# Transposes between the products of the second pair, and where the block sums of layer 0 run, in a two-layer hybrid decoder

## The chip, the cores and the metric

The kernel runs on one core of one Trainium2 chip. The metric is the device time of that core in microseconds; the time before is the median of three runs. A profile of one further execution comes with it. In the profile PE is TensorE, DVE is VectorE, ACT is ScalarE, POOL is GpSimd, SP is SyncE (here a DMA queue). L234 is line 234 of the kernel before.

## What is computed

A trunk of two layers over 1024 tokens of width 1024, in float32. Layer 0 mixes tokens with an RG-LRU block, layer 1 with RWKV-7; each mixer is followed by a cross-attention into 256 memory tokens and by a squared-ReLU MLP:

```python
def reference(x, mem, ...):
    mem_n = rms_norm(mem, mem_norm)
    for i in range(DEPTH):
        g = ln_gains[i]
        hn = rms_norm(x, g[0])
        t = rglru_mixer(hn, ...) if i % N_MIXERS == 0 else rwkv7_mixer(hn, ...)
        x = x + rms_norm(t, g[1])
        c = mem_cross_attention(rms_norm(x, g[2]), mem_n, c_w_q[i], c_w_kv[i], c_w_o[i])
        x = x + rms_norm(c, g[3])
        m = sqrelu_mlp(rms_norm(x, g[4]), m_w_up[i], m_w_down[i])
        x = x + rms_norm(m, g[5])
    return x

def mem_cross_attention(h, mem_n, w_q, w_kv, w_o):
    q = (h @ w_q).reshape(B, S, MEM_HEADS, MEM_HEAD_DIM)
    ...

def sqrelu_mlp(h, w_up, w_down):
    return jnp.square(jax.nn.relu(h @ w_up)) @ w_down
```

## The kernel before

**Arithmetic.** Each float32 product is made of three matmuls on operands that are split in a high and a low half (`mm3`, L314 to L320: high by high L318, high by low L319, low by high L320). A split (`split`, L228 to L235) is a cast on ACT (L233) and a subtraction on DVE (L234) for the low half; of a whole unit of 128 x 1024 it is one instruction of each.

**Phases.** A projection whose result leaves with tokens on the partitions is a `tphase`: eight token tiles of 128, for each one 48 matmuls of 512 columns, then `post`, which runs the tail (post-norm, residual, pre-norm of the next block: L327 on ACT, L329 and L331 on POOL, L647, L648 and L655 on DVE). The pre-normed tiles are collected in `xs`; when four are there, a step that transposes them is put into `self.later`, and `catch_up` runs what waits there.

**The 7-product projections.** The query projections of both layers (`c_w_q`, 4 pairs of output tiles) and the up projections of both MLPs (`m_w_up`, 16 pairs) go through `cphase`. It takes the activations as 2 x 2 blocks and computes a pair with seven products of 12 matmuls each instead of eight. `combine_in` makes the operands from the activations: for each half `hf` of the tokens it transposes four tiles, eight groups `k` of four transposes (L384), evacuates each group with the norm's gain (L387 on DVE for k = 1 and 3, L389 on ACT), and splits blocks. The half `hf` = 0 gives b11 and b21. With `hf` = 1 come the block sums t1 = b12 - b11, t2 = b22 - t1, t3 = b11 - t2 and t4 = b21 - t2 (L415; two units each, so eight subtractions) and the splits of t1, t2, t3, b22 and t4. `combine_w` makes the four weight sums of a pair on POOL (L433, L434) and splits them. `make` does that ahead of time: the tphase of a cross-attention calls it behind its tiles 4 and 5 (`MAKE`), so that the MLP's first two pairs find their weights made.

`begin` runs p1 (with b11, into the bank x, copied by ACT, L474) and p2 (with b21, into z, added by DVE, L476). `finish` takes the made weights or calls `combine_w`. The first two pairs run in `together`: begin and finish of both, then `mid`, then p5, p6, p7, p3 and p4, each for both pairs. p5 reads t1, p6 t2, p7 t3, p3 b22 and p4 t4; p6 and p5 are copied by ACT (L485, L490), p7 and p3 added by DVE (L494, L498). For the first two pairs `mid` is `second_half`: it changes the PSUM layout to two pools of four banks and calls `catch_up`, which runs `combine_in` for `hf` = 1, 32 transposes and all sums.

**Layer 0's query projection is different.** There `xattn` first runs the rest of `memkv` (keys and values of layer 1's memory: each step 48 matmuls of 256 columns, with two splits of weights). `self.held` is a list then, and `combine_in` puts the five steps t1, t2, t3, b22, t4 into it, with the subtractions on POOL; after each of five `memkv` steps one of them is run.

**Order.** The program is written out once; the framework then puts each engine's instructions in order by a planner, by program order among those that it reckons ready. Tiles come from pools: 45 units of 128 x 1024 in SBUF (`BUFS`), PSUM banks by `bank(n)`, which takes pool n modulo the number of pools. Weights are fetched in the order of a plan; `depth` and `ahead` say how many units are split and loaded ahead, and loads go through SP's queue (L245 for pairs of projection weights, L253 for rows).

Of the kernel before, what the change touches and what calls it, by code (L numbers as in the profile page):

```python
# [9 lines left out]
AF = mybir.ActivationFunctionType  # L10
ALU = mybir.AluOpType
# [16 lines left out]
MAKE = (4, 5)  # L28
D = 1024
KT = 8  # L30
# [19 lines left out]
class Net:  # L50
# [322 lines left out]
    def combine_in(self, xs, hf, g, B):  # L373

        nc = self.nc
        raw = B.setdefault("raw", {})
        for k in range(KT):
            if k % 2 == 0:
                t = raw[hf, k // 2] = self.unit()
                pair = self.halves()  # L380
            o = slice((k % 2) * 512, (k % 2) * 512 + 512)
            p = pair[k % 2]
            for i, x in enumerate(xs):
                nc.tensor.transpose(p[:, i * 128:i * 128 + 128], x[:, k * 128:k * 128 + 128], self.ident)  # L384
            gc = self.colt[:, g + k:g + k + 1]
            if k in (1, 3):
                nc.vector.tensor_scalar(t[:, o], p, gc, None, ALU.mult)  # L387
            else:
                nc.scalar.activation(t[:, o], p, AF.Copy, scale=gc)  # L389

        def parts(name, ts, big=False):
            if big:
                z = self.half_big([4, 1024], F32R)
                st = [z[:, i, :] for i in range(4)]
            else:
                st = [self.unit(F32R) for _ in range(4)]
            for i, t in enumerate(ts):
                self.split(t, st[i], st[2 + i])
            at = lambda o, k: st[o + k // 2][:, (k % 2) * 512:(k % 2) * 512 + 512]
            B[name] = [(at(0, k), at(2, k)) for k in range(4)]  # L400

        r = lambda h, j: [raw[h, 2 * j + i] for i in range(2)]
        if hf == 0:
            parts("b11", r(0, 0), True)
            parts("b21", r(0, 1), True)
            return
        b11, b21, b12, b22 = r(0, 0), r(0, 1), r(1, 0), r(1, 1)
        del B["raw"]
        t2 = []

        def sums(name, to, x, y):
            if name == "t2":
                to.extend(self.unit() for _ in range(2))
            for o, m, n in zip(to, x, y):
                eng.tensor_tensor(o, m, n, ALU.subtract)  # L415
            parts(name, to)

        eng = nc.vector if self.held is None else nc.gpsimd
        steps = [lambda: sums("t1", b12, b12, b11), lambda: sums("t2", t2, b22, b12), lambda: sums("t3", b11, t2, b11),
                 lambda: parts("b22", b22), lambda: sums("t4", b21, b21, t2)]  # L420
        if self.held is None:
            for step in steps:
                step()
        else:
            self.held += steps

    def combine_w(self, two, first):

# [30 lines left out]
    def cphase(self, w, n, B, func, evac, then=None, ahead=2):  # L459

        nc = self.nc
        a, b = slice(0, 512), slice(512, 1024)
        st = {}


        place = lambda i: 0 if i < ahead else (i + 1) % 2

        def begin(i):
            two, first = self.made[i][:2] if i in self.made else self.take(("w", w, i))
            h, l = first  # L470
            x, z = self.bank(place(i)), self.bank(place(i))
            c0, c1 = self.unit(), self.unit()
            self.product(x, (h[:, a], l[:, a]), B["b11"], True, False)
            nc.scalar.copy(c0[:, a], x)  # L474
            self.product(z, (h[:, b], l[:, b]), B["b21"], True, True)
            nc.vector.tensor_add(c0[:, a], c0[:, a], z)  # L476
            st[i] = x, c0, c1, two, first

        def finish(i):
            x, c0, c1, two, first = st[i]  # L480
            st[i] = x, [], c0, c1, self.made.pop(i)[2] if i in self.made else self.combine_w(two, first)

        def p6(x, y, c0, c1, A, at):
            self.product(x, A["s2"], B["t2"], False, False)
            nc.scalar.copy(c0[:, b], x)  # L485

        def p5(x, y, c0, c1, A, at):
            y.append(self.bank(1 if at < ahead else place(at)))
            self.product(y[0], A["s1"], B["t1"], True, False)
            nc.scalar.copy(c1[:, b], y[0])  # L490

        def p7(x, y, c0, c1, A, at):
            self.product(x, A["s3"], B["t3"], False, False)
            nc.vector.tensor_add(c1[:, b], c1[:, b], x)  # L494

        def p3(x, y, c0, c1, A, at):
            self.product(y[0], A["s4"], B["b22"], False, True)
            nc.vector.tensor_add(c0[:, b], c0[:, b], y[0])  # L498

        def p4(x, y, c0, c1, A, at):  # L500
            self.product(x, A["a22"], B["t4"], False, True)
            nc.scalar.activation(c1[:, a], x, func or AF.Copy)

        def end(i):
            c0, c1 = st.pop(i)[2:4]
            if func is not None:
                nc.scalar.activation(c0, c0, func)
                nc.scalar.activation(c1[:, b], c1[:, b], func)
            behind.append(evac(i, c0, c1))


        behind = []

        def rest():
            while behind:
                behind.pop(0)()


        def narrow(i):
            if i >= n - 2:  # L520
                self.depth, self.ahead = 2 * (n - 1 - i), 0

        def together(two, mid=lambda: None):
            for i in two:
                narrow(i)
                begin(i)
                finish(i)
                if then and i == n - 2:
                    then[0]()
            mid()  # L530
            for step in (p5, p6, p7, p3, p4):
                for i in two:
                    step(*st[i], i)
                if then and step is p7 and two[-1] == n - 1:
                    with self.behind():
                        then[1]()
            for i in two:
                end(i)

        def second_half():  # L540
            self.psum_layout("banks")
            self.catch_up()

        together(range(ahead), second_half)
        for i in range(ahead, n - 2 if then else n):
            narrow(i)
            begin(i)
            finish(i)
            rest()
            for step in (p6, p5, p7, p3, p4):  # L550
                step(*st[i], i)
            end(i)
        if then:
            together(range(n - 2, n), rest)
        return rest


# [314 lines left out]
    def xattn(self, layer, xt, post, mid):  # L872
# [13 lines left out]
        if layer == 0:  # L886

            self.memkv(1, 3)
            self.held = []
            self.catch_up()  # L890
            for _ in range(5):
                self.memkv(1, 1)
                self.held.pop(0)()
            self.held = None
        self.kv_flush()
        self.depth, self.ahead = UP
# [331 lines left out]
        yield from rwkv_lora_weights(self, parts, out[-1])  # L1228


def rwkv(self, X, xt, lw_wa, lw_g, post):
    nc, I = self.nc, self.I
    mm = nc.tensor.matmul
    hgd = self.dram([128, 1024])
# [13 lines left out]
    raw = self.unit()  # L1248
# [571 lines left out]
    for q in range(4):  # L1820
        for h in range(2):
            rows.append([w[(2 * q + pp) * 128 + h * 64:(2 * q + pp) * 128 + h * 64 + 64, :] for pp in range(2)])
    self.tphase(rows, lambda tt: z[tt], post)


def network(net, I, out):
    x = [I["x"][0]] + [net.dram([1024, 1024]) for _ in range(5)] + [out[0]]
    early = []
    g = lambda l, i: I["ln_gains"][l, i]
    net.memory()  # L1830
    net.memkv(0, START[0])
    net.cols_fill(net.nc.gpsimd, 256)
    xt = net.head(x[0], net.lncol(0, 0), beside=START[1:])
    net.memory_out()
    net.memkv(0, 8 - sum(START))
    net.cols_fill(net.nc.gpsimd, 328)
    post, nxt = net.tail(g(0, 1), x[0], x[1], net.lncol(0, 2), combine=True)
    net.rglru(xt, post)
    for l in range(2):
        if l == 1:  # L1840
            xt = nxt
            post, nxt = net.tail(g(1, 1), x[3], x[4], net.lncol(1, 2), combine=True)
            rwkv(net, raw, xt, *early, post)
        post, xt = net.tail(g(l, 3), x[3 * l + 1], x[3 * l + 2], net.lncol(l, 4), combine=True)
        net.xattn(l, nxt, post, lambda tt: tt in MAKE and net.make(I["m_w_up"][l], MAKE.index(tt)))
        raw = []
        if l == 0:
            post, nxt = net.tail(g(0, 5), x[2], x[3], net.lncol(1, 0), raw=raw)
        else:
            post, nxt = net.tail(g(1, 5), x[5], x[6], None, last=True)  # L1850
        net.mlp(l, xt, raw, post, [rwkv_early(net, early)] if l == 0 else None)
# [21 lines left out]
```

## Time and profile before

| | |
|---|---|
| median of 3 runs | 2918.43 us (2918.1 to 2918.5) |
| the profiled execution, its own time | 2919.01 us |
| its span, first to last instruction | 2917.3 us |
| mean granted TensorE clock | 0.987 |
| PE busy | 2810.0 us |
| DVE busy | 1844.2 us |
| ACT busy | 1421.5 us |
| POOL busy | 929.3 us |
| matmuls | 16955 |
| HBM traffic | 143 GB/s over the span |

A row of the timeline reads: start in us from the span's start, duration, engine, line, operation, output <- input by the program's names, shapes and count, and in brackets the idle time of the engine just before and what ended it. In a row of waits stand the waiting engine and line, whom it waited for, the sum in us, the times and the longest. In the view by stretches each row is a stretch, its length, then the busy time of each engine with the number of its instructions, the granted clock, the share of the DMA engines and GB/s. A group row gives line, engine, operation, shapes and count, then busy us and mean ns, then the idle time ahead of it. Matmuls overlap in the pipeline, so the pace is read from the distance between their starts, not from their durations.

### The profile page before, as it was taken

The page shows a single profiled execution, that of the slowest core. Times are in us where ns is not written, and L with a number is a line of the kernel's source. Part 1 is how long each engine was busy: PE and PEld are TensorE (multiplying, and loading weights), DVE is VectorE, ACT ScalarE, POOL GpSimd, SP SyncE. Part 2 cuts the span into 40 slices and gives each one's busy share as a digit, 9 for nine tenths or more (in the row PEclk, how much of TensorE's full clock was granted, in tenths as well). Part 3 has the DMA queues.
Part 4 walks back from the last instruction along what each step waited for, and adds up shares of the span by engine and source line. Part 5 has one row for each costly group of instructions (what it writes and reads, how often), then busy time and mean ns, then how long its engine had stood idle before and what let it go on. Part 6 is the DMA issues. An engine that isn't in the chain of part 4 may idle for free.

```text
span 2917.3 us, 42725 instructions
## 1 busy us (share of the span) xinstructions
PE 2810.0 (96%) x16955; PEld 2342.2 (80%) x16955; DVE 1844.2 (63%) x1987; ACT 1421.5 (49%) x2195; POOL 929.3 (32%) x970
## 2 busy tenths in 40 slices
PE   7999999999999999999999899999899999999998
PEld 6888788887888888887878677888688788888886
DVE  5577566657455577887676624773765645567778
ACT  6465354545444543347561534553554544454333
POOL 2000144023666500012287113851402376650001
PEclk9999999999999999999999999999999999999999
DMA  8212342323444654442657798952232354464443
GB/s 258 78 46 73 108 160 68 104 81 102 150 153 155 221 183 158 146 144 73 176 139 219 213 226 238 240 131 94 62 106 80 102 162 145 147 238 162 157 173 115
DMA packets 383591, 421.91 MB, mean 145 GB/s; under 512 B 91184, under 2 KB 294176, under 8 KB 383392
## 3 DMA queue, kind: packets, MB, share of 16 engines
q1 hardware_dynamic: 371360, 379.19, 43.2%
q0 software_dynamic: 11568, 39.41, 3.7%
q8 instruction: 133, 2.18, 0.3%
q14 instruction: 66, 0.54, 0.1%
q10 hardware_dynamic: 464, 0.59, 0.1%
HBM read 283.79 MB, written 134.74 MB: 143 GB/s over the span
## 4 chain that ended last, share of the span: by engine, by line
PE 81%; DVE 5%; DMA 4%; issue 4%; ACT 3%; POOL 3%; SPq 1%; DVEq 0%; POOLq 0%; ACTq 0%
PE q L318 16%; PE q L320 16%; PE q L319 16%; PE p L318 8%; PE p L320 8%; PE p L319 8%; DVE u L234 2%; DMA u<-d 1%; PE q L1642 1%; DMA u<-in_b_w_rkv 1%; ACT u L233 1%; POOL u L1401 1%; POOL w L1399 1%; PE q L1535 1%; PE q L384 1%
## 5 line engine op out<-in xcount | busy, mean ns | idle before, releaser
L234 DVE TENSOR_TENSOR u<-u,u 128x1024 fp32r<-128x1024 f32 (+1 forms) x594 | 817.5, 1409 | 363.9 <-ACT u L233 341.8
L233 ACT CAST u<-u 128x1024 fp32r<-128x1024 f32 (+1 forms) x594 | 582.3, 1019 | 426.3 <-DVE u L1032 224.7
L318 PE MATMUL q<-u,u 128*128 128x512 f32 (+2 forms) x1984 | 760.0, 386 | 13.8 <-ACT u L233 10.9
L319 PE MATMUL q<-u,u 128*128 128x512 f32 (+2 forms) x1984 | 760.4, 384 | 8.5 <-DVE u L234 7.7
L320 PE MATMUL q<-u,u 128*128 128x512 f32 (+2 forms) x1984 | 753.9, 383 | 0.8 <-DVE u L234 0.8
L318 PE MATMUL p<-u,u 128*128 128x512 f32 (+1 forms) x1472 | 557.2, 381 | 16.3 <-ACT u L233 5.6
L319 PE MATMUL p<-u,u 128*128 128x512 f32 (+1 forms) x1472 | 554.5, 377 | 3.9 <-DVE u L234 3.9
L320 PE MATMUL p<-u,u 128*128 128x512 f32 (+1 forms) x1472 | 552.5, 376 | 3.2 <-DVE u L234 3.2
L318 PEld LDWEIGHTS q<-u,u 128*128 128x128 f32 (+1 forms) x1984 | 373.9, 189 | 90.8 <-ACT u L233 13.0
L329 POOL TENSOR_SCALAR s<-s 128x1 f32<-128x1 f32 x98 | 40.0, 409 | 1273.4 <-ACT u L327 1271.9
L319 PEld LDWEIGHTS q<-u,u 128*128 128x128 f32 (+1 forms) x1984 | 374.3, 189 | 82.4 <-DVE u L234 10.8
L320 PEld LDWEIGHTS q<-u,u 128*128 128x128 f32 (+1 forms) x1984 | 374.2, 189 | 73.9 <-DVE u L234 1.0
L318 PEld LDWEIGHTS p<-u,u 128*128 128x128 f32 x1472 | 281.6, 191 | 70.3 <-ACT u L233 11.8
L319 PEld LDWEIGHTS p<-u,u 128*128 128x128 f32 x1472 | 281.7, 191 | 55.8 <-DVE u L234 7.0
L320 PEld LDWEIGHTS p<-u,u 128*128 128x128 f32 x1472 | 281.1, 191 | 54.7 <-DVE u L234 5.0
L433 POOL TENSOR_TENSOR u<-u,u 128x512 f32<-128x512 f32 x120 | 192.1, 1605 | 10.1 <-PE q L319 5.1
L1090 DVE TENSOR_TENSOR z<-z,q 128x512 f32<-128x512 f32 x192 | 130.4, 682 | 81.1 <-PE q L320 81.1
L320 PE MATMUL q<-z,u 128*128 128x512 f32 x320 | 124.9, 392 | 3.9 <-DVE u L234 3.9
L319 PE MATMUL q<-z,u 128*128 128x512 f32 x320 | 125.0, 391 | 0.0
L318 PE MATMUL q<-z,u 128*128 128x512 f32 x320 | 124.8, 391 | 0.0
L434 POOL TENSOR_TENSOR u<-u 128x512 f32<-128x512 f32 x40 | 62.4, 1559 | 139.3 <-DVE u L234 82.4
L647 DVE SCALAR_TENSOR_TENSOR u<-p,s,u 128x1024 f32<-128x1024 f32 x24 | 30.8, 1284 | 112.0 <-ACT u L233 76.2
(248 smaller groups left out, 3362.5 us busy)
## 6 DMA issues: line engine op xcount, KB each, us to landing
u<-d SPq DMA_DIRECT2D x194, 512.0 KB, 4.7
d<-u SPq DMA_DIRECT2D x109, 512.0 KB, 3.4
d<-u POOLq DMA_DIRECT2D x68, 512.0 KB, 3.3
d<-u SPq DMA_DIRECT2D x132, 256.0 KB, 3.5
u<-in_m_w_up SPq DMA_DIRECT2D x64, 512.0 KB, 5.4
u<-in_m_w_down SPq DMA_DIRECT2D x64, 512.0 KB, 7.9
u<-in_c_w_kv SPq DMA_DIRECT2D x32, 512.0 KB, 6.6
u<-in_b_w_rkv SPq DMA_DIRECT2D x24, 512.0 KB, 6.2
```

Source lines behind the costliest of these rows:

```text
L233: self.nc.scalar.copy(hv, src)
L234: (eng or self.nc.vector).tensor_tensor(lv, src, hv, ALU.subtract)
L318: mm(o, ah, bh, start=first, stop=False, **kw)
L319: mm(o, ah, bl, start=False, stop=False, **kw)
L320: mm(o, al, bh, start=False, stop=last, **kw)
L329: nc.gpsimd.tensor_scalar(v, ss, 1.0 / n, eps, ALU.mult, ALU.add)
L384: nc.tensor.transpose(p[:, i * 128:i * 128 + 128], x[:, k * 128:k * 128 + 128], self.ident)
L433: sub = lambda o, x, y: nc.gpsimd.tensor_tensor(o, x, y, ALU.subtract)
L434: nc.gpsimd.tensor_tensor(s[:, a], f1[:, a], f1[:, b], ALU.add)
L647: nc.vector.scalar_tensor_tensor(o, src, r, gb, ALU.mult, ALU.mult)
L1090: nc.vector.tensor_add(to_, to_, o)
L1399: eng.tensor_tensor(tv, xv_[:, 0:n, s:s + 1].broadcast_to([128, n, m]), Lv[:, s:s + 1, s + 1:].broadcast_to([128, n, m]), ALU.mult)
```

## The change

Four edits. In `combine_in` the transposes and evacuations are split in two groups, k = 0 to 3 and k = 4 to 7, and where `held` is None t1's subtraction and split are written between them; in the second half of the tokens both PSUM buffers of a group's pair come from `bank(1)`. In `cphase` the step `mid` moves from behind `begin` and `finish` of both pairs into the second pair's `begin`, between p1 and p2. In layer 0's `xattn` the block sums run on DVE, only t1 and t2 between the `memkv` steps (behind the first and the third), and t3, b22 and t4 go to `self.later`, so that `second_half` runs them. The tphase at the end of `rwkv` calls `make` for the first two pairs of layer 1's `c_w_q` behind its tiles 4 and 5.

```diff
     def combine_in(self, xs, hf, g, B):
...
-        for k in range(KT):
-            if k % 2 == 0:
-                t = raw[hf, k // 2] = self.unit()
-                pair = self.halves()
...
+        def turned(ks):
+            for k in ks:
+                if k % 2 == 0:
+                    t = raw[hf, k // 2] = self.unit()
+                    pair = [self.bank(1) for _ in range(2)] if hf else self.halves()
...
+        turned(range(4))
         if hf == 0:
+            turned(range(4, 8))
             parts("b11", r(0, 0), True)
             parts("b21", r(0, 1), True)
             return
-        b11, b21, b12, b22 = r(0, 0), r(0, 1), r(1, 0), r(1, 1)
-        del B["raw"]
...
             for o, m, n in zip(to, x, y):
-                eng.tensor_tensor(o, m, n, ALU.subtract)
+                nc.vector.tensor_tensor(o, m, n, ALU.subtract)
             parts(name, to)
-        eng = nc.vector if self.held is None else nc.gpsimd
-        steps = [lambda: sums("t1", b12, b12, b11), lambda: sums("t2", t2, b22, b12), lambda: sums("t3", b11, t2, b11),
+        b11, b21, b12 = r(0, 0), r(0, 1), r(1, 0)
+        if self.held is None:
+            sums("t1", b12, b12, b11)
+        turned(range(4, 8))
+        b22 = r(1, 1)
+        del B["raw"]
+        steps = [lambda: sums("t2", t2, b22, b12), lambda: sums("t3", b11, t2, b11),
                  lambda: parts("b22", b22), lambda: sums("t4", b21, b21, t2)]
         if self.held is None:
             for step in steps:
                 step()
         else:
-            self.held += steps
+            self.held += [lambda: sums("t1", b12, b12, b11)] + steps
...
-        def begin(i):
+        def begin(i, mid=lambda: None):
...
             nc.scalar.copy(c0[:, a], x)
+            mid()
             self.product(z, (h[:, b], l[:, b]), B["b21"], True, True)
...
-        def together(two, mid=lambda: None):
+        def together(two, mid=lambda: None, late=lambda: None):
             for i in two:
                 narrow(i)
-                begin(i)
+                begin(i, mid if i == two[-1] else lambda: None)
                 finish(i)
                 if then and i == n - 2:
                     then[0]()
-            mid()
+            late()
...
-            together(range(n - 2, n), rest)
+            together(range(n - 2, n), late=rest)
...
-            for _ in range(5):
+            for i in range(5):
                 self.memkv(1, 1)
-                self.held.pop(0)()
+                if i in (0, 2):
+                    self.held.pop(0)()
+            self.later += self.held
             self.held = None
...
-def rwkv(self, X, xt, lw_wa, lw_g, post):
+def rwkv(self, X, xt, lw_wa, lw_g, post, mid):
...
-    self.tphase(rows, lambda tt: z[tt], post)
+    self.tphase(rows, lambda tt: z[tt], post, mid)
...
-            rwkv(net, raw, xt, *early, post)
+            rwkv(net, raw, xt, *early, post, lambda tt: tt in MAKE and net.make(I["c_w_q"][1], MAKE.index(tt)))
```

More of the change, by code (lines that the diff above doesn't have):

```diff
@@ L376, in combine_in @@
         raw = B.setdefault("raw", {})
-        for k in range(KT):
-            if k % 2 == 0:
-                t = raw[hf, k // 2] = self.unit()
-                pair = self.halves()
[L381 to L389, printed above, removed]
+        def turned(ks):
[3 more added lines that the diff above has]
+                    pair = [self.bank(1) for _ in range(2)] if hf else self.halves()
+                o = slice((k % 2) * 512, (k % 2) * 512 + 512)
+                p = pair[k % 2]
+                for i, x in enumerate(xs):
+                    nc.tensor.transpose(p[:, i * 128:i * 128 + 128], x[:, k * 128:k * 128 + 128], self.ident)
+                gc = self.colt[:, g + k:g + k + 1]
+                if k in (1, 3):
+                    nc.vector.tensor_scalar(t[:, o], p, gc, None, ALU.mult)
+                else:
+                    nc.scalar.activation(t[:, o], p, AF.Copy, scale=gc)
         def parts(name, ts, big=False):
```

## The prediction

> **What bounds the kernel now.** I read the page first, then PE by stretches, the list of waits, then the timeline of each engine around the four places that the diff touches. I call such a place a seam: the end of a tphase, the start of the next cphase.
>
> ```profile
> PE 2810.0 (96%) x16955; PEld 2342.2 (80%) x16955; DVE 1844.2 (63%) x1987; ACT 1421.5 (49%) x2195; POOL 929.3 (32%) x970
> ```
>
> TensorE is the bound nearly everywhere; VectorE's 63% is an average that hides the seams. So the change is worth what it takes from TensorE's stalls there. The view by stretches, one around each seam and a stall-free one for the pace:
>
> ```profile
> core 0: us, PE busy (x) PEld busy (x) DVE busy (x) ACT busy (x) POOL busy (x), PEclk, DMA share, GB/s
> 418.64:456.67 38.03, 31.25 (x244) 30.84 (x242) 34.37 (x17) 19.82 (x24) 25.88 (x10) 0.91 0.41 123
> 683.94:731.83 47.89, 44.29 (x202) 35.97 (x200) 33.52 (x33) 28.91 (x38) 11.97 (x11) 0.96 0.39 117
> 2041.26:2137.79 96.53, 85.72 (x386) 70.69 (x385) 70.25 (x61) 47.27 (x61) 31.76 (x22) 0.96 0.29 91
> 2283.07:2330.96 47.89, 44.47 (x201) 35.72 (x200) 33.52 (x33) 28.91 (x38) 11.97 (x11) 0.96 0.39 117
> 1000.00:1200.00 200.00, 200.00 (x884) 165.62 (x883) 158.27 (x167) 90.93 (x100) 17.40 (x12) 1.00 0.51 172
> ```
>
> The last row gives the pace: 200.00 / 884 = 0.226 us for a 512-wide matmul, 2.71 us for a product of 12. The waits of the first seam, the longest of the third, then TensorE's rows in the second seam and in the first:
>
> ```profile
> PE q L319 <- DVE u L234: 6.8, 2, 5.8
> PE q L320 <- DVE u L234: 1.8, 2, 1.0
> PE q L318 <- ACT u L485: 0.7, 1, 0.7
> PE q L384 <- DVE u L476: 5.7, 1, 5.7
> ```
>
> ```profile
> 694.83 3.22 PE L384 MATMUL q<-ident,u 128*128 128x128 f32 x28
> 698.39 0.66 PE L384 MATMUL q<-ident,u 128*128 128x128 f32 x4 [0.34 <-ACT u L389]
> 701.63 0.73 PE L318 MATMUL q<-u,u 128*128 128x512 f32 x2 [2.59 <-ACT u L233]
> ...
> 703.97 0.63 PE L319 MATMUL q<-u,u 128*128 128x512 f32 x1
> 704.39 0.63 PE L320 MATMUL q<-u,u 128*128 128x512 f32 x1
> ```
>
> ```profile
> 415.65 3.24 PE L384 MATMUL q<-ident,u 128*128 128x128 f32 x26
> ...
> 418.85 0.28 PE L319 MATMUL q<-u,u 128*128 128x256 f32 x1
> 418.96 0.29 PE L320 MATMUL q<-u,u 128*128 128x256 f32 x1
> ```
>
> The reader is to see two losses: the wait itself, and what follows it. From 703.97 to 704.39 matmuls start 0.42 us apart, nearly twice 0.226: after a stall of a few us the granted clock is halved for some us (the stretches' PEclk is 0.91 and 0.96). 32 transposes take 32 x 3.22 / 28, with the tail left out about 3.4 us. A 256-wide matmul is 0.12 us.
>
> What each seam loses now, its length less the matmuls at pace (one neighbour at either border left out):
> - Seam 1, layer 0's query projection, with memkv's matmuls ahead of it: 38.03 - 241 x 0.12 = 9.1 us; with the 1.0 and 0.7 us of the waits in its first products 10.8.
> - Seam 2, layer 0's MLP: 47.89 - 168 x 0.226 - 3.4 = 6.5. Seam 4, layer 1's MLP: the same 47.89, so 6.5.
> - Seam 3, layer 1's query projection: 386 less 32 transposes and 18 matmuls of scores is 336: 96.53 - 76.0 - 3.4 - 18 x 0.12 = 14.9.
>
> Together 38.7 us: no more can be had.
>
> **The change part by part.**
>
> *Seams 2 and 4: transposes between p1 and p2 of the second pair, t1 split ahead of the last four transposes' evacuations.* Nothing is added: 32 transposes, 8 subtractions, 10 splits before and after. VectorE's and ACT's rows in seam 2:
>
> ```profile
> 691.40 0.76 DVE L655 TENSOR_SCALAR u<-u,s 128x1024 f32<-128x1024 f32 x1 [0.38 <-POOL s L331]
> ...
> 696.12 1.41 DVE L387 TENSOR_SCALAR u<-q,colt 128x512 f32<-128x512 f32 x2 [0.34 <-PE q L384]
> 697.45 2.35 DVE L415 TENSOR_TENSOR u<-u,u 128x1024 f32<-128x1024 f32 x2
> 701.62 2.36 DVE L234 TENSOR_TENSOR u<-u,u 128x1024 fp32r<-128x1024 f32 x2 [1.81 <-ACT u L233]
> ...
> 711.84 1.21 DVE L234 TENSOR_TENSOR u<-u,u 128x1024 fp32r<-128x1024 f32 x1
> ```
>
> ```profile
> 697.65 3.00 ACT L389 ACTIVATE u<-q,colt 128x512 f32<-128x512 f32 x5 [0.95 <-PE q L384]
> 700.52 2.01 ACT L233 CAST u<-u 128x1024 fp32r<-128x1024 f32 x2
> ```
>
> The transposes need the normed last tile, ready at 691.40 + 0.76 = 692.2. The second pair's p1 ends at 683.94 + 36 x 0.226 = 692.1. So they can start at T0 = 692.2, 2.6 us earlier than at 694.83, and hardly hold PE. Then p2 runs and p5 can start at T0 + 3.4 + 2.7 = T0 + 6.1. Is t1 ready by then? Now: first evacuations 1.3 us behind the transposes' start, subtractions done at +5.0, the casts at +5.7 only because ACT still had five evacuations in hand until 700.6, p5 at +6.8. With the casts ahead of those, the first one starts near +3.8 (0.7 for the evacuation and 1.2 for the subtraction behind +1.3, and handovers), ends at +4.8, its low half on VectorE at +6.0: p5 starts without a wait. In the order of now p5 would wait 0.7. The stall of 2.59, the 0.53 and 0.34 behind it and the half clock go.
>
> What is late next is t2. Its second low half ends at 711.84 + 1.2 = 713.0, that is +18.2; p6's eighth matmul, which reads it, would come at T0 + 6.1 + 5.4 + 1.6 = +13.1. With VectorE's order unchanged but for the 1.81 us that it waited for ACT it comes at +16.4: a stall of 3.3 us. In program order (t2's splits ahead of t3's subtractions) it ends near +12: none. The queue's whole work, 18 instructions at 1.15 and two evacuations, is 22 us, done near T0 + 24, with t4 needed at T0 + 6.1 + 8 x 2.7 = +28. I take 1.5 us lost, nearer the program order, since the casts no longer wait: gain 6.5 - 1.5 = 5.0 in each seam, bounds 2.5 and 6.5.
>
> Both buffers of a transpose pair now come from the second pool of four banks, in which the fifth transpose group waits for the first evacuation, 0.7 us long: about 0.3 us, within the 1.5.
>
> *Seam 3: the same, and make() for c_w_q in the tphase ahead of it.* Now the first two pairs' combinations, 8 subtractions or additions on POOL and their splits, lie in the seam and delay the last tile's norm:
>
> ```profile
> 2053.76 1.78 DVE L655 TENSOR_SCALAR u<-u,s 128x1024 f32<-128x1024 f32 x1 [0.44 <-POOL s L331]
> ```
>
> It ends at 2055.5, 14.3 us after the tphase's last product (2041.26), against 692.2 - 683.9 = 8.3 in seam 2, where the weights are made in the tphase. Making them there costs TensorE what it costs in layer 0's tphase, stretch 634 to 684:
>
> ```profile
> L320 PE MATMUL p<-u,u 128*128 128x512 f32 x69 | 26.9, 390 | 0.0
> ...
> L433 POOL TENSOR_TENSOR u<-u,u 128x512 f32<-128x512 f32 x6 | 9.1, 1509 | 0.2
> ```
>
> No idle time before the matmuls beside six of POOL's instructions: nothing. The loads themselves do not move, they are issued ahead of the tphase on SP's queue:
>
> ```profile
> 1935.62 1.49 SPq L245 DMA_DIRECT2D u<-in_c_w_q  x2
> ```
>
> Pairs 2 and 3, now prefetched, are loaded behind the first products instead, as in the MLPs, some 25 us ahead of use. So seam 3 becomes seam 2: 14.9 - 1.5, less 1 for the tighter slots (the recurrence's output is still in up to two units): gain 12.4, bounds 6 (weights late all the same) and 14.9.
>
> *Seam 1: sums of layer 0 on VectorE, three of five steps later.* Stretch 417 to 442, by groups, and stretch 697 to 720, where POOL is idle for most of it:
>
> ```profile
> L234 DVE TENSOR_TENSOR u<-u,u 128x1024 fp32r<-128x1024 f32 x7 | 22.4, 3261 | 2.5 <-ACT u L233 2.5
> L415 POOL TENSOR_TENSOR u<-u,u 128x1024 f32<-128x1024 f32 x8 | 24.7, 3115 | 9.0 <-ACT u L389 9.0
> ```
>
> ```profile
> L234 DVE TENSOR_TENSOR u<-u,u 128x1024 fp32r<-128x1024 f32 x10 | 11.6, 1214 | 1.8 <-ACT u L233 1.8
> L415 DVE TENSOR_TENSOR u<-u,u 128x1024 f32<-128x1024 f32 x8 | 9.3, 1214 | 0.0
> ```
>
> Beside POOL's eight sums a split's low half takes 3.26 us, alone 1.21; that is the 5.8 us wait. On VectorE the eight sums cost 9.3 and spare POOL 24.7. Under memkv's 28.9 us remain 10 low halves for its weights, 2 for the projection's, 4 sums and 4 low halves of t1 and t2: 20 x 1.21 = 24 us. It fits; I leave 1 of the 9.1. Moved behind the second p1 are 10 instructions (t3, b22, t4) on top of six low halves of combined weights, all beside POOL's combinations, where four low halves take 7.87:
>
> ```profile
> 464.65 7.87 DVE L234 TENSOR_TENSOR u<-u,u 128x1024 fp32r<-128x1024 f32 x4
> ```
>
> Up to 16 x 1.97 = 31 us, against 12 products x 2.71 = 32.5 from the projection's start to t4's use. Nearly full: p5's second weights or t4 can come late. Bounds 0 and 6; I take 2.5, since half of it can run without POOL beside it. Gain 10.8 - 1 - 2.5 = 7.3, bounds 3.8 and 10.8.
>
> Sum: 5.0 + 5.0 + 12.4 + 7.3 = 29.7 us. The profiled execution took 2919.0 us, 0.6 over the median of 2918.43; the forecast is 2918.4 - 29.7 = 2888.7.
>
> **The rivals.**
> - *VectorE's queue is the bound in the seams.* For it: its 33.5 of 47.9 us busy, nearly all in the second half. All low bounds: 2.5 + 2.5 + 6 + 3.8 = 14.8, so 2904.
> - *The transposes stay where they were.* The planner orders PE's queue by what it reckons ready; if it reckons the last tile late, p2 goes first. 692.2 against 692.1 is close. Then seams 2 and 4 win only the earlier casts, 1 each, seam 3 14.9 - 6.5 = 8.4 and 1, seam 1 7.3: 18.7, so 2900.
> - *The transposes cost the clock.* Put between products, 3.4 us of them could halve the clock for p2, 16 matmuls 0.2 us longer: 3 us in each of three seams, so 2898. Against it: behind the 26 transposes at 415.65 the next matmuls start 0.11 us apart, full pace. The Trainium skill, TensorE: Matmul & The Clock Gate, says in Part 4 that a transpose doesn't count as busy in the way a matmul does, and in Part 1 that one idle window of about 3.4 us halves the clock: by that rule this would be the time. The trace agrees on the halving after a stall, not on 26 transposes; with 32 no row shows it.
> - *Slots run out in the tphase ahead of seam 3* (the other side). Of 45 units I count 16 for w_o, 6 for split tiles, 14 for the made weights, up to 8 for tiles and 2 for the recurrence's output: 46. If short, a tile's norm waits for the one before, and its chain of 8.3 us stands bare, with 2 us of half clock behind it. From three tiles on that eats the gain; at four it is 41 us: 2930. Against it: layer 0's tphase runs with 44 and no idle.
>
> **How the numbers follow.** Forecast 0.58, own range 2880 (all upper bounds, 38.7) to 2897; VectorE the bound 0.12; transposes unmoved 0.10; clock 0.08; slots 0.07; gain taken back by an order elsewhere, no change, 0.05. The range 2879 to 2909 leaves out the last two. A measurement of this kernel tells about 0.2%, 5.8 us, from no change: faster 0.88, same 0.05, slower 0.07.
>
> **What would show it.** Right: transposes before the second p2 in seams 2 to 4, at most 1.5 us of waits from p5 on, no rows 0.42 us apart behind them; no POOL combination between 2041 and 2060; memkv without the 5.8 us wait, and low halves there at 1.2 us. Wrong: a wait of p6 or p4 on VectorE of over 3 us, a half-clock p2, or TensorE idle in the tphase ahead of seam 3.

## The result, and the profile after

The changed kernel takes 2898.07 us (median of four, 2895.14 to 2899.91) against 2918.47 for the kernel before on the same chip: a ratio of 0.9926, 95% interval 0.9914 to 0.9939, so 20.4 us of the 29.7 forecast. The time lies inside the range and is clearly faster; it is 9.4 us over the number and 1.1 over the range of the likeliest case alone (2880 to 2897), and what the seams did is not what that case says. The profiled execution took 2897.32 us, its span 2895.6 (before 2917.3).

To see where the time went, the timeline of TensorE is cut at fixed rows. Seam 1 runs here from the end of layer 0's first tphase to a row in the scores that waits alike in every kernel (586.69 before), seams 2 and 4 from the first product to the third pair, seam 3 from its first product to the same row of layer 1's scores:

```profile
2185.83 1.14 PE L932 MATMUL q<-ident,u 128*128 128x128 f32 x8 [1.38 <-ACT z L945]
```
```profile
2165.21 1.14 PE L942 MATMUL q<-ident,u 128*128 128x128 f32 x8 [1.38 <-ACT z L955]
```

The first is of the kernel before, the second of the changed one. "Middle" is what lies between seams 2 and 3, the first MLP's rest and the recurrence; the stretches not listed agree within 0.2 us, but for the start (up to 1.6), the end behind the last matmul (up to 0.6) and the stretch behind seam 4 in e2 and e3 (below). The expectations measure seams 1 and 3 to the end of their projection, some 50 us earlier (seam 1 139.9 before and 132.5 changed, seam 3 96.3 and 88.0). All in us, one profiled execution each, the kernels of the experiments with their labels:

| kernel | seam 1 | seam 2 | seam 3 | seam 4 | sum of seams | middle |
|---|---|---|---|---|---|---|
| before | 190.25 | 47.89 | 144.57 | 47.89 | 430.60 | 1309.43 |
| changed | 182.17 | 47.32 | 136.30 | 46.92 | 412.71 | 1304.98 |
| e1_y_bank | 182.33 | 46.49 | 134.77 | 46.49 | 410.08 | 1304.50 |
| e2_p2_behind | 182.60 | 44.37 | 132.60 | 44.41 | 403.98 | 1304.65 |
| e3_both | 183.47 | 44.38 | 132.62 | 44.38 | 404.85 | 1304.28 |
| e4_t1_late | 182.27 | 47.84 | 135.30 | 46.96 | 412.37 | 1308.48 |
| p1_make_alone | 190.07 | 47.94 | 136.12 | 47.89 | 422.02 | 1305.27 |
| p2_layer0_alone | 180.99 | 47.93 | 145.54 | 47.90 | 422.36 | 1313.16 |
| p3_seams_alone | 190.13 | 47.36 | 151.02 | 46.73 | 435.24 | 1308.79 |
| p4_no_seams | 181.26 | 47.89 | 136.16 | 47.94 | 413.25 | 1304.23 |
| e5_p2_behind_first | 182.07 | 44.39 | 132.58 | 44.38 | 403.42 | 1306.88 |
| e6_t2_first | 182.05 | 43.11 | 131.35 | 43.11 | 399.62 | 1308.09 |
| r_after_again | 182.12 | 47.32 | 135.24 | 46.92 | 411.60 | 1302.86 |
| r_before_again | 190.41 | 47.90 | 144.43 | 47.90 | 430.64 | 1306.33 |

The changed kernel gains 8.1 in seam 1 (forecast 7.3), 0.6 and 1.0 in seams 2 and 4 (5.0 each), 8.3 in seam 3 (12.4): 17.9 us. 4.4 more lie in the middle, where nothing was forecast. The engines' totals and the stretches of the seams in the changed kernel:

```profile
PE 2804.9 (97%) x16955; PEld 2341.9 (81%) x16955; DVE 1834.2 (63%) x1995; ACT 1421.7 (49%) x2195; POOL 907.3 (31%) x962
```
```profile
418.50:446.30 27.80, 26.24 (x212) 25.36 (x211) 22.73 (x21) 16.96 (x21) 6.20 (x1) 1.00 0.62 180
676.61:723.93 47.32, 43.70 (x202) 35.83 (x200) 33.97 (x33) 29.03 (x38) 11.99 (x11) 0.96 0.39 119
2028.91:2116.90 87.99, 84.66 (x385) 70.23 (x384) 55.78 (x54) 40.98 (x54) 18.04 (x14) 0.96 0.32 100
2262.44:2309.36 46.92, 43.59 (x202) 35.98 (x200) 34.32 (x33) 29.12 (x38) 11.01 (x11) 0.96 0.40 120
```

In memkv's stretch the clock is 1.00 (0.91 before), while seams 2 to 4 still show 0.96: the stall with its half clock is still there. TensorE's rows in seam 2, without the single full-pace matmuls between them:

```profile
684.78 1.48 PE L386 MATMUL q<-ident,u 128*128 128x128 f32 x12
...
688.17 0.60 PE L386 MATMUL q<-ident,u 128*128 128x128 f32 x4
...
689.31 1.94 PE L386 MATMUL q<-ident,u 128*128 128x128 f32 x16
694.58 0.80 PE L318 MATMUL q<-u,u 128*128 128x512 f32 x1 [3.33 <-ACT u L391]
695.18 0.63 PE L319 MATMUL q<-u,u 128*128 128x512 f32 x1
695.60 0.63 PE L320 MATMUL q<-u,u 128*128 128x512 f32 x1
```

Twelve transposes of the three ready tiles come at 684.78. Nine of p2's matmuls follow, then, at 688.17, the last tile's four; the other three of p2, and the last sixteen. p5 waits 3.33 us and starts at half pace (0.42 us apart). The two engines that p5 waits for, DVE and then ACT:

```profile
684.08 0.75 DVE L663 TENSOR_SCALAR u<-u,s 128x1024 f32<-128x1024 f32 x1 [0.39 <-POOL s L331]
688.59 1.41 DVE L389 TENSOR_SCALAR u<-q,colt 128x512 f32<-128x512 f32 x2 [3.76 <-PE q L386]
689.92 1.22 DVE L417 TENSOR_TENSOR u<-u,u 128x1024 f32<-128x1024 f32 x1
691.05 0.68 DVE L484 TENSOR_TENSOR u<-u,q 128x512 f32<-128x512 f32 x1
691.65 1.22 DVE L417 TENSOR_TENSOR u<-u,u 128x1024 f32<-128x1024 f32 x1
```
```profile
692.90 1.04 ACT L233 CAST u<-u 128x1024 fp32r<-128x1024 f32 x1 [0.69 <-DVE u L417]
693.85 2.41 ACT L391 ACTIVATE u<-q,colt 128x512 f32<-128x512 f32 x4
```

The last tile was ready at 684.08 + 0.75 = 684.8, yet its first transposes stand behind nine of p2's matmuls in TensorE's queue and start 3.4 us later. VectorE idles 3.76 us for them, the second sum of t1 stands behind p2's addition (L484), the cast behind that sum, and the evacuations of k = 4 to 7 behind the cast. p5's bank comes from the pool of those groups, so p5 waits for an evacuation that waits for t1. Seams 3 and 4 show the same wait of 3.33.

### The profile page after: what moved, and what is told of

Read it like the earlier page. It is cut to its first block, busy times and chain, and to the rows that moved or that the text cites. A ratio compares the mean times of both kernels' runs of the same rounds, so it can differ in the third digit from the quotient of the medians.

```text
span 2895.6 us, 42717 instructions
## 1 busy us (share of the span) xinstructions
PE 2804.9 (97%) x16955; PEld 2341.9 (81%) x16955; DVE 1834.2 (63%) x1995; ACT 1421.7 (49%) x2195; POOL 907.3 (31%) x962
## 4 chain that ended last, share of the span: by engine, by line
PE 86%; DVE 5%; ACT 3%; DMA 2%; issue 2%; SPq 1%; POOL 0%; DVEq 0%; POOLq 0%; ACTq 0%
PE q L318 17%; PE q L320 17%; PE q L319 17%; PE p L318 9%; PE p L320 9%; PE p L319 9%; DVE u L234 1%; PE q L1652 1%; ACT u L233 1%; PE q L386 1%; DMA u<-in_b_w_rkv 1%; DVE u L1199 1%; PE q L1545 1%; PE q L1769 1%; ACT u L930 1%
## 5 line engine op out<-in xcount | busy, mean ns | idle before, releaser
L234 DVE TENSOR_TENSOR u<-u,u 128x1024 fp32r<-128x1024 f32 (+1 forms) x594 | 799.3, 1378 | 353.9 <-ACT u L233 331.8
L318 PEld LDWEIGHTS q<-u,u 128*128 128x128 f32 (+1 forms) x1984 | 373.6, 189 | 92.8 <-ACT u L391 10.9
L440 POOL TENSOR_TENSOR u<-u,u 128x512 f32<-128x512 f32 x120 | 189.1, 1579 | 9.0 <-PE q L319 5.1
L441 POOL TENSOR_TENSOR u<-u 128x512 f32<-128x512 f32 x40 | 70.0, 1749 | 166.1 <-DVE u L234 63.7
L997 POOL TENSOR_TENSOR u<-u,u 128x512 f32<-128x512 f32 x32 | 44.2, 1381 | 177.0 <-ACT u L986 159.8
```

The source lines that it names most:

```text
L234: (eng or self.nc.vector).tensor_tensor(lv, src, hv, ALU.subtract)
L318: mm(o, ah, bh, start=first, stop=False, **kw)
L440: sub = lambda o, x, y: nc.gpsimd.tensor_tensor(o, x, y, ALU.subtract)
L441: nc.gpsimd.tensor_tensor(s[:, a], f1[:, a], f1[:, b], ALU.add)
L997: tt(s1, r21, r22, ALU.add)
```

## The experiments

**Order or bank: four kernels on one chip.** Each starts from the changed kernel. The kernel before had a median of 2918.14 us there.

e1, p5's bank from the first pool:

```diff
-            y.append(self.bank(1 if at < ahead else place(at)))
+            y.append(self.bank(place(at)))
```

> p5's bank for the first two pairs comes from the first pool (p2's bank, free by then), not from the pool that the transposes fill; all else as in the changed kernel. Theory A (the changed kernel's 3.3 us wait of p5 in seams 2 to 4 is for a PSUM bank that ACT empties only behind t1's casts, but the last tile's late transposes hold t1 back nearly as long): p5 starts when t1's first cast is done, 692.2 instead of 694.6 us in seam 2, and then waits for t1's low half until 694.0, so 1 us or less per seam is won, at most 5 us in all with a shorter slow clock: 2893 to 2898. Theory B (the bank is the whole of it): the wait of 3.3 us and the slow clock behind it go, 4 to 5 us per seam, 2883 to 2886.

Measured: 2900.28 us, ratio 0.9945 (0.9926 to 0.9963). Seams 2 and 4 are 0.8 and 0.4 us shorter than in the changed kernel, no more: theory A in the seams, though the median lies over its 2893 to 2898. The wait for the bank is gone, but p5 then waits for t1, first 1.02 us for the cast and then 1.06 for the low half; the rest of the first row is p6's. In seam 2:

```profile
PE q L319 <- DVE u L234: 2.6, 3, 1.2
PE q L318 <- ACT u L233: 1.0, 1, 1.0
```

e2, p2 behind the transposes in the planner's order (`behind` issues what it holds after the last instruction so far of each engine):

```diff
             mid()
-            self.product(z, (h[:, b], l[:, b]), B["b21"], True, True)
+            with self.behind():
+                self.product(z, (h[:, b], l[:, b]), B["b21"], True, True)
```

> The second pair's p2 is put behind all 32 transposes on TensorE's queue; banks as in the changed kernel. Theory A (the loss is the order on TensorE: 12 of p2's matmuls stand among the transposes, ahead of the last tile's, and leave nothing between the transposes and p5): the last tile's transposes start 3.3 us earlier, p2's 2.7 us cover t1's chain, the wait at p5 falls from 3.3 to under 1 us and the half clock goes: 4 to 5 us in each of seams 2 to 4, 2883 to 2887. Rival (VectorE's queue is the bound behind the transposes): the wait moves from p5 to p6, and a seam wins 1.5 us or less: 2893 or more.

Measured: 2894.61 us, ratio 0.9921 (0.9906 to 0.9936). Seams 2, 3 and 4 are 3.0, 3.7 and 2.5 us shorter than in the changed kernel. That lies between the two theories: p5's wait is gone, as theory A has it, but TensorE now waits 1.2 us for VectorE in seam 2, the rival's wait, and the time is in the rival's range (2893 or more) and not in theory A's. `behind` also holds the last pairs of each projection here; the stretch from seam 4 to the last matmul grew from 573.4 to 575.0 us. The median alone can't tell this kernel from the changed one (0.9926 on another chip); e5 below can.

e3, both edits:

> Both: p2 behind the transposes and p5's bank from the first pool. Theory A: no wait at p5, 0.7 us per seam better than p2 behind the transposes alone: 2881 to 2885. Rival (VectorE's queue): no better than p2 behind the transposes alone, waits of p6 on VectorE of 1 to 3 us.

Measured: 2895.51 us, ratio 0.9926 (0.9910 to 0.9942); the seams of e2 within 0.03 us in 2 to 4, so no better than e2, as the rival has it, and 1.5 us of waits for VectorE in seam 2. Once the order is right, p5's bank doesn't matter: the order is the cause, the bank the place where it showed.

e4, t1's sums behind all transposes and evacuations:

```diff
-        if self.held is None:
-            sums("t1", b12, b12, b11)
         turned(range(4, 8))
+        b11, b21, b12 = r(0, 0), r(0, 1), r(1, 0)
+        if self.held is None:
+            sums("t1", b12, b12, b11)
```

> The changed kernel with one part undone: t1's subtraction and split are written behind the last four transposes again, so that ACT empties all groups first and casts t1 afterwards. Theory A: p5's bank is free earlier but t1's casts come at 692.9 instead of 691.2 in seam 2; p5 waits for t1 instead of its bank until 694 to 695: within 1 us per seam of the changed kernel, 2896 to 2901. Theory B (the bank is all): the wait at p5 falls by 2 us or more per seam, 2888 to 2892.

Measured: 2902.77 us, ratio 0.9953 (0.9936 to 0.9969). Seam 2 is 0.5 us longer, seam 4 the same, seam 3 1.0 shorter, which is no more than two profiles of the changed kernel differ by there (136.30 and 135.24). So with the order as built, taking t1 first is worth half a us at most: theory A in the seams, with a time 1.8 us over its range. On this chip all four medians gain 2.7 to 3.1 us less than the kernels' seams do, so these four are compared by their seams.

**The parts alone, and the order mended for the first pairs.** On this chip the kernel before had 2919.49. p1 is the kernel before with `make` in the tphase ahead of seam 3:

```diff
-    self.tphase(rows, lambda tt: z[tt], post)
+    self.tphase(rows, lambda tt: z[tt], post, mid)
```

> The kernel before, with one part of the change: the first weights of layer 1's query projection are combined in the tphase ahead of it. Transposes, sums and layer 0 stay as before. The changed kernel's seam 3 is 88.0 us long against 96.3 before. Theory 1, nearly all of that comes from the weights, since the planner kept p2 among the transposes and the other edit there brought the MLPs only 0.6 and 1.0 us: seam 3 at 87.4 to 89, seams 2 and 4 at 47.9 as before, seam 1 at 139.9, the time some 8 us under before (2909 to 2911). Theory 2, the edits need each other, since the transposes between p1 and p2 are what uses the earlier tile: seam 3 at 91 to 93, the time 3 to 5 us under before. Theory 3, slots run out in the tphase: TensorE idle there, the time 10 us or more over before. The stretch between seams 2 and 3, 1309.4 us before and 1305.0 in the changed kernel: if making the weights there is what reorders it, it is near 1305 here too and 4.5 us more come off.

Measured: 2908.68 us, ratio 0.9965 (0.9952 to 0.9978). Seam 3 is 8.45 us shorter, all that the whole change brings there: theory 1. The middle came out at 1305.27, near the 1305 named for the case that the weights are what shortens it. No slots run out. That holds for the changed kernel too, whose tphase ahead of seam 3 shows POOL's combinations and a full TensorE (the view by stretches, then two groups of its second half):

```profile
1935.00:2028.50 93.50, 93.50 (x423) 77.62 (x424) 52.82 (x48) 40.76 (x71) 32.75 (x38) 0.97 0.22 74
```
```profile
L320 PE MATMUL p<-u,u 128*128 128x512 f32 x67 | 26.1, 389 | 0.0
...
L440 POOL TENSOR_TENSOR u<-u,u 128x512 f32<-128x512 f32 x6 | 9.0, 1507 | 0.2
```

p2 is the kernel before with layer 0's sums on VectorE and three steps later:

```diff
-        eng = nc.vector if self.held is None else nc.gpsimd
+        eng = nc.vector
...
-            for _ in range(5):
+            for i in range(5):
                 self.memkv(1, 1)
-                self.held.pop(0)()
+                if i in (0, 2):
+                    self.held.pop(0)()
+            self.later += self.held
```

> The kernel before, with the layer-0 part alone: sums of layer 0 on VectorE, those of t1 and t2 between memkv's steps, the other three steps later. Theory 1, the loss in seam 1 is POOL's sums slowing VectorE's splits: seam 1 at 132 to 133 us as in the changed kernel (139.9 before), memkv without the wait of 5.7 us, seams 2 to 4 as before (47.9, 96.3, 47.9), the time 7.4 us under before (2911). Theory 2, the gain there comes from the split of the first sum and the order of the transposes too: seam 1 at 135 to 138, the time 2 to 5 us under. The stretch between seams 2 and 3 at 1309.4 if this part doesn't reach it, 1305 if it does.

Measured: 2912.07 us, ratio 0.9980 (0.9971 to 0.9990). Seam 1 is 9.3 us shorter, 1.2 more than in the whole change; theory 1. The kernel has both edits at once, the engine and the three later steps, but all eight sums ran under memkv in it as before (the last done at 442.5 us, the projection's first product at 443.8), so the later place of the three steps can have done little. The median gained less than the seam, and its profile's middle is 3.7 us longer, the longest of all (below).

p3 is the transposes and the first sum's split alone (the changed kernel without `make` ahead of seam 3 and with layer 0 as before):

> The changed kernel without the weights made ahead of seam 3 and without the layer-0 part: the transposes between p1 and p2 and the first sum's split alone. Theory 1, p2's matmuls among the transposes leave this part nearly nothing: seams 2 and 4 at 46.9 to 47.3 us (47.9 before), seam 3 at 95 to 96.3, since its last tile comes 14 us late whatever the order of p2, the time 2 to 3 us under before (2915 to 2917), which is no change that can be measured. Theory 2, it is this part that shortens seam 3: seam 3 at 90 to 92, the time 6 to 8 us under before. Seam 1 at 139.9 either way. The stretch between seams 2 and 3 at 1305 if this part is what reorders it.

Measured: 2921.13 us, ratio 1.0006 (0.9998 to 1.0015). Seams 2 and 4 gain 0.5 and 1.2 as expected, but seam 3 is 6.45 us longer than before, which neither theory had. The waits of seam 3, in this kernel and in the kernel before:

```profile
PE q L319 <- DVE u L234: 5.3, 2, 3.3
PE q L318 <- ACT u L391: 3.3, 1, 3.3
PE q L320 <- DVE u L234: 1.8, 1, 1.8
PE q L386 <- DVE u L389: 0.8, 2, 0.6
PE q L318 <- ACT u L494: 0.7, 1, 0.7
PE q L386 <- ACT u L391: 0.5, 1, 0.5
```
```profile
PE q L384 <- DVE u L476: 5.7, 1, 5.7
PE q L318 <- ACT u L233: 3.4, 1, 3.4
PE q L320 <- DVE u L234: 1.8, 1, 1.8
```

The waits add up to 12.4 us there and to 10.9 before, only 1.5 more, but they come as eight stalls instead of three, and more matmuls run at half pace: 27 of seam 3's start 0.40 to 0.45 us after the one before, against 6. The stretch's granted clock is 0.90 against 0.96.

```profile
2040.66:2140.00 99.34, 87.06 (x367) 69.62 (x366) 67.96 (x61) 46.92 (x61) 31.51 (x22) 0.90 0.28 89
```

e5 is the changed kernel with p2 behind the transposes for the second pair only:

```diff
+            with self.behind() if i == ahead - 1 else ExitStack():
+                self.product(z, (h[:, b], l[:, b]), B["b21"], True, True)
```

> The changed kernel with p2 of the second pair put behind the transposes in the planner's order; the other pairs as in the changed kernel. Theory 1, the order alone costs the seams what they fell short by: seams 2, 3 and 4 at 44.4, 84.3 and 44.4 us as with p2 behind in every pair, and the stretch behind seam 4 back at 573.4 (it was 575.0 with p2 behind in every pair), so 9.1 us under the changed kernel's span of 2895.6 (2886.5), a time of 2887 to 2890. Theory 2, the 1.6 us behind seam 4 came with the shorter seam, not with the last pairs: the stretch stays at 575.0 and the span at 2888. Theory 3, the clock halves behind 32 transposes: p2's matmuls 0.42 us apart, seams 2 and 4 at 46 or more.

Measured: 2889.06 us, ratio 0.9895 (0.9883 to 0.9908). Seams 44.39, 132.58 and 44.38, the stretch behind seam 4 573.41: theory 1 on each of these. The span was 2889.1 instead of 2886.5, since the middle came out 1.9 us longer and the start 0.6. What is left in seam 2:

```profile
PE q L319 <- DVE u L234: 1.1, 2, 0.7
PE q L386 <- ACT u L391: 0.5, 1, 0.5
```

The 1.1 is p6, which waits for t2's low halves; the 0.5 the fifth transpose group, which waits for a bank.

**VectorE's order, the seams taken out, and two kernels again.** On this chip the kernel before had 2918.74. e6 is e5 with t3, b22 and t4 behind t2:

```diff
-            for step in steps:
-                step()
+            steps.pop(0)()
+            with self.behind():
+                for step in steps:
+                    step()
```

> The changed kernel with p2 of the second pair behind the transposes, and t2's low halves ahead of t3's subtractions, of b22's parts and of t4 on VectorE (t3, b22 and t4 put behind t2 in the planner's order). With p2 behind alone, p6 still waits twice in each of seams 2 to 4: 0.73 and 0.40 us for t2's low halves, the first done at 699.3. Theory 1, VectorE's order is what holds p6: both waits gone, seams 2 and 4 at 43.2 to 43.4 us (44.4 with p2 behind alone), seam 3 from its first product to the fixed row in the scores at 131.4 (132.6), some 3.4 us in all. Theory 2, the eight subtractions and sixteen splits are simply too much for the time: the wait moves to p7, which reads t3, or to p3 or p4, and the seams stay at 44.2 to 44.5. The rest of the kernel as with p2 behind alone.

Measured: 2886.79 us (2885.28 to 2890.19), ratio 0.9893 (0.9878 to 0.9909); the changed kernel's median on the same chip is 2895.71. Seams 43.11, 131.35 and 43.11, 3.8 us less in all than in e5: theory 1, by a little more. Its waits in seam 2, and its stretches of seams 2 and 4, at full clock:

```profile
PE q L386 <- ACT u L391: 0.5, 1, 0.5
PE q L319 <- DVE u L234: 0.2, 1, 0.2
```
```profile
676.86:719.97 43.11, 42.43 (x201) 34.81 (x200) 32.99 (x33) 28.84 (x38) 10.98 (x11) 1.00 0.43 130
...
2256.66:2299.77 43.11, 42.42 (x201) 34.81 (x200) 33.00 (x33) 28.83 (x38) 10.98 (x11) 1.00 0.44 130
```

p4 is the change without its seams' part, p1 and p2 together:

> The changed kernel without the transposes between p1 and p2 and without the first sum's split: the weights made ahead of seam 3, and layer 0's sums on VectorE with three steps later. Theory 1, the three parts' effects in the seams add up as they did alone, and the seams' part as built brings only 0.6 and 1.0 us in seams 2 and 4: from the end of layer 0's first tphase to the scores 181 us, as with the layer-0 part alone (182.2 in the changed kernel); seams 2 and 4 at 47.9; seam 3 to the scores' fixed row 136.1, as with the weights alone (136.3); all that outside the middle stretch 0 to 1 us over the changed kernel. Theory 2, the seams' part is needed for the others to bring their gain in full: seam 3 to the scores at 139 or more, the whole 3 us or more over the changed kernel. The middle stretch, which differed by up to 9 us between kernels in which nothing there was edited (1304.3 to 1313.2), is left out of both.

Measured: 2898.97 us, ratio 0.9936 (0.9921 to 0.9952), against 0.9926 (0.9909 to 0.9942) for the whole change in the same comparison. Its seams sum to 413.25, the changed kernel's to 412.71 and 411.60. Theory 1: the parts add up, and moving the transposes, as the planner ordered it, brought nothing that a time can tell.

The changed kernel and the kernel before once more:

> The changed kernel once more, for a second execution of it in a profile. The stretch between seams 2 and 3 was 1304.98 us in its first and 1309.43 in the kernel before; 4.4 us of the measured gain lie there, in which the forecast had none. Theory 1, the stretch varies from execution to execution, with the waits on a transfer and on VectorE in the recurrence's front part: it comes out 2 us or more away from 1305.0, while every other stretch repeats within 0.5 us. Theory 2, the change orders the stretch otherwise and the 4.4 us are its own: 1304.5 to 1305.5 again.

> The kernel before once more, for a second execution of it in a profile. Theory 1, the stretch between seams 2 and 3 varies from execution to execution: it comes out 2 us or more away from 1309.43. Theory 2, the stretch is the kernel's own: 1309 to 1310 again, while seams 1 to 4 repeat within 0.3 us under both.

Measured: 2895.71 us, ratio 0.9926 (0.9909 to 0.9942), and 2917.07, ratio 0.9994 (0.9983 to 1.0006). The middle came out 2.1 us shorter in the changed kernel and 3.1 shorter in the kernel before: theory 1 in both. Seams 1, 2 and 4 repeat within 0.2 us; seam 3 of the changed kernel differed by 1.1, more than expected, so less than that isn't read from seam 3. One wait of the middle that moves much, in the order before, before again, changed, changed again:

```profile
PE q L1438 <- DMA u<-d: 0.4, 1, 0.4
```
```profile
PE q L1438 <- DMA u<-d: 3.3, 1, 3.3
```
```profile
PE q L1448 <- DMA u<-d: 3.5, 1, 3.5
```
```profile
PE q L1448 <- DMA u<-d: 1.7, 1, 1.7
```

This wait on a transfer is 0.4 or 3.3 us in two executions of one kernel. It isn't what sets the middle's length, for in the kernel before the longer wait falls in the shorter middle. Over all fourteen profiles the middle lies between 1302.9 and 1313.2.

## Why the prediction was right, and where not

*Direction and range* were right because of seam 1 and because of the weights made ahead of seam 3, the two parts with a loss measured in the trace and a cover that the trace showed. They alone make a kernel with 17.4 us less in its seams (p4, 430.60 - 413.25).

*Seam 1*, forecast 7.3, gained 8.1. POOL's sums are gone from it, VectorE's rows of the stretch 417 to 446 show the price that was used (1.21), and the wait of 5.8 us is gone; TensorE's waits from the end of the first tphase to the end of the projection are in the second block:

```profile
L234 DVE TENSOR_TENSOR u<-u,u 128x1024 fp32r<-128x1024 f32 x12 | 14.2, 1222 | 5.0 <-ACT u L233 5.0
L417 DVE TENSOR_TENSOR u<-u,u 128x1024 f32<-128x1024 f32 x8 | 9.4, 1221 | 0.3 <-ACT u L391 0.2
```
```profile
PE q L318 <- ACT u L233: 1.6, 1, 1.6
PE q L320 <- DVE u L234: 0.8, 1, 0.8
PE q L318 <- ACT u L493: 0.7, 1, 0.7
```

The 0.8 is under memkv, the 1.6 a cast at the projection's first product. The 2.5 us for the moved steps was too much, since the sums did not move: the first block has all eight of them under memkv (x8), where the planner ran t3's and t4's too, the last done at 443.4 us, ahead of the projection's first product at 444.7. No wait of the projection is put down to VectorE, and behind its first product there is only the 0.7, for a copy of ACT's. With the old order of the transposes the seam gains 9.3 (p2).

*Seams 2 and 4*, forecast 5.0, gained 0.6 and 1.0. The step that failed is the order on TensorE, all transposes at T0 and "Then p2 runs". T0 was right: the last tile was ready 8.2 us after the first product, forecast 8.3. But p2 was not behind the transposes; the planner put nine of its matmuls ahead of the last tile's. "The transposes stay where they were", a rival with a chance of 0.10, came true in half: the first twelve moved, the last twenty stayed behind nine or all twelve of p2's matmuls. That the planner reckoned the last tile late, as the rival says, fits this order, but no run shows what it reckoned. The rival's 1 us for each of these seams fits the 0.6 and 1.0, though its reason, the earlier casts, is worth half a us at most (e4). Its 2900 for the whole is 1.9 from the measured time, in part by luck: 4.4 us of the profile's gain lie in the middle, for which it has nothing. The step behind it, p5 at T0 + 6.1, or seam start + 14.4, came within 0.9 us with the order mended: in e6 p5 starts at 692.16, 15.3 behind 676.86. The 0.9 us are the 0.51 of the fifth group's wait (forecast 0.3) and handovers.

*t2 as the next to be late*, 1.5 us taken in each seam: in e5, p6 waited 1.1, and with t2's low halves first (e6) seams 2 and 4 shrank by 1.28 and 1.27. This term was right in kind and nearly in size, though in the changed kernel itself, where p5 starts late, p6 doesn't wait. The program order that the prediction leaned towards is not what the planner chose; VectorE ran t3's and t4's sums ahead of t2's low halves or between them.

*Seam 3*, forecast 12.4, gained 8.3, all from the weights (p1: 8.45). "So seam 3 becomes seam 2" was right, for it then lost the same 3.33 us in the same place: with the order mended it gains 12.0 (e5), with t2 first 13.2 (e6). What the prediction did not see is that the transposes' move needs the weights: alone it makes seam 3 6.45 us longer (p3).

*The sum.* The forecast's 29.7 us is the sum for an order between those of e5 and e6. e5, with p2 behind the transposes, gains 8.2 + 3.5 + 12.0 + 3.5 = 27.2 in the seams; e6, with t2 first on VectorE too, 8.2 + 4.8 + 13.2 + 4.8 = 31.0, and its ratio of 0.9893 on 2918.74 is 31.2 us. That e6 comes so close is in part luck: the 1.5 us for t2 are gone from it, and 1.7 us of other losses stand in their place (seam 2's 43.11 less the 38.0 of matmuls and 3.4 of transposes that were reckoned).

*The other rivals.* "The transposes cost the clock" falls: in e6 all 32 stand between p1 and p2, with 0.51 us of idle in them, and p2 follows at full pace, 12 matmuls from 689.17 to p5 at 692.16:

```profile
685.03 1.91 PE L386 MATMUL q<-ident,u 128*128 128x128 f32 x16
687.45 1.97 PE L386 MATMUL q<-ident,u 128*128 128x128 f32 x16 [0.51 <-ACT u L391]
689.17 0.48 PE L318 MATMUL q<-z,u 128*128 128x512 f32 x1
...
692.16 0.50 PE L318 MATMUL q<-u,u 128*128 128x512 f32 x1
```

The rule of the Trainium skill's page TensorE: Matmul & The Clock Gate, Part 4, that a transpose doesn't count as busy in the way a matmul does, thus has no effect that this run shows. The halving after one idle window (Part 1) agrees in kind with the changed kernel, where p5's matmuls start 0.42 us apart behind 3.33 us of idle. The page's window is about 3.4 us, and 3.33 us, or 2.59 in the kernel before, were enough here; whether the transposes ahead of such a stall count towards the window, no run shows. "Slots run out" did not happen (p1). "VectorE's queue is the bound": in e6 TensorE waits 0.2 us for the same VectorE work in seam 2, so it was its order and not its amount.

*The middle*, 4.4 us of the span's 21.7, is the part without a cause that is shown. It varies by 2 to 3 us between executions of one kernel. Two profiles of each give 1309.4 and 1306.3 before, 1305.0 and 1302.9 changed: 4.0 us between the means, no more than chance of that size can make. All fourteen profiles hint at the weights, which are made in this stretch: the ten kernels that make them there have a mean of 1305.4 (1302.9 to 1308.5), the four others 1309.4 (1306.3 to 1313.2). But the two ranges overlap, so whether the change shortens the middle stays open.

## What to carry to other kernels

A step moved in the program is moved on the chip only if the order that is really issued says so: where a planner decides, forecast the order first, and look for a close call between two ready times. Where an edit gives an engine something to start on earlier, check that the last operand comes earlier too; half-ready work placed among other work turned three stalls of seam 3 into eight, with more matmuls at half pace. And measure the parts alone and together: here the move of the transposes brought nothing that a time can tell until one edit fixed the order, and then 9 us in the seams.

## What the runs showed of the hardware

The clock stayed up through 32 transposes between matmuls, 1.00 over the stretch, while one idle time of 3.33 us was followed by 3.1 us at half pace in seam 2 of the changed kernel and by 5.7 in its seam 3. VectorE's two-input operation on 1024 elements, 3.26 us beside POOL's eight sums before, takes 1.22 beside a single POOL combination, and that one spans 9.0 us there (a POOL span is rough), where six combinations in the tphase ahead of seam 3 take 1.5 each:

```profile
L441 POOL TENSOR_TENSOR u<-u 128x512 f32<-128x512 f32 x1 | 9.0, 9001 | 31.3 <-DMA d<-u 31.3
```
